# Regrouping the block-attention scores of layer 1: both chunks of a section in one group, later transposes

## The chip, the cores and the metric

The kernel runs on one core of a Trainium2 chip. The metric is the device time of one execution in microseconds, as the median over several runs. The engines are named as the profile names them: PE (TensorE matmul), PEld (its weight loads), DVE (VectorE), ACT (ScalarE), POOL (GpSimd), SP (SyncE, which issues the weight loads from memory).

## The reference

A decoder trunk of two layers on 256 positions of width 1024. Layer 0 mixes tokens by dilated sliding-window attention, layer 1 by MoBA block attention; each is followed by a gated feed-forward net with a causal convolution. The change is in layer 1's attention:

```python
SEQ = 256; N_HEADS = 16; HEAD_DIM = 64; MOBA_BLOCK = 256
def mixer_moba(h, w_qkv, q_gain, k_gain, w_o, cos, sin):
    qkv = (h @ w_qkv).reshape(B, S, 3, N_HEADS, HEAD_DIM)
    q = apply_partial_rope(rmsnorm(qkv[:, :, 0], q_gain), cos, sin)
    k = apply_partial_rope(rmsnorm(qkv[:, :, 1], k_gain), cos, sin)
    v = qkv[:, :, 2]
    ...
    s_own = jnp.einsum('hqd,hkd->hqk', qc, k_own) * ATTN_SCALE   # own block only: fully past blocks do not exist here
    s_own = jnp.where((kpos[None, :] <= qpos[:, None])[None], s_own, -jnp.inf)
    p = jax.nn.softmax(...)
    return o + jnp.einsum('hqk,hkd->hqd', p[..., n_sel:], v_own)
```

With 256 positions there is a single block of 256, so layer 1 is plain causal attention with 16 heads.

## The kernel before

**Tiling.** The positions form two chunks of 128 rows. The 16 heads are worked in four sections of four heads. Weights stream in as units; each unit is split by ACT into a rounded part `whi` (L109) and by DVE into the rest `wlo` (L117), and each product takes three matmuls of 128x512 (`mm3`, L456 to L458): x-high by `whi`, x-low by `whi`, x-high by `wlo`.

**Turns.** The program is an order written out by hand. `turn` runs one step `fn` of weight matmuls and, around it, what earlier steps have put into the tables `first`, `pre`, `mid` and `post` for this turn number. A turn issues, in this order: up to two `whi` splits, the entries of `first`, one `wlo`, the entries of `pre`, the other `wlo`, the matmuls of `fn`, the entries of `post`. `at(table, d, f)` puts `f` into the turn `d` later. Each engine executes its own instructions in the order in which they are issued. In the attention a turn has 12 weight matmuls, in the output projection of layer 1 (`out_proj`) 6.

**Buffers.** Tiles of one name share a fixed number of buffers: PSUM banks `S` 4, `acc` 3, `O` 1; in SBUF `sm` 2, `qk` 5, `pT` 4. A new tile takes the buffer that has been free longest, and its first writer waits for that buffer's last reader.

**One section of layer 1.** The product gives q and k of a chunk (`qk_block`); ACT squares and copies it (L539, L533), DVE sums and rotates (`head_sums`, `factors`), PE transposes it (`transpose`, L580), ACT copies it (L610) and DVE makes the low parts (`second_parts`, L616, L618). Then, for a group of heads of chunk `c`:

- `step_A`: score matmuls into two S banks (L676 for chunk 0, 128 keys; L682 for chunk 1, 256 keys)
- `step_E`: masked maxima (L708) and bias (L715) on DVE, exponentials on ACT (L717), into `sm`
- `step_R`: division by the sums on DVE (L722, L724)
- `step_T`: transposes on PE into S banks (L732); four for a group of 512 columns
- `step_V`: copies by ACT into `pT` (L739)
- `step_C`: matmuls with v into `O` for the whole section (L764); in the turn after, `split_T` brings `O` into `aT` as high part (ACT, L444) and low part (DVE, L445)

Chunk 0 is one group of four heads, chunk 1 two groups of two. Counted from layer 1's first turn, sections start in turns 0, 8, 12 and 16 and the output projection in turn 24. Scores of chunk 0 stand behind the matmuls of turns 6, 13, 18 and 23, those of chunk 1 in turns 8 and 10, 15 and 17, 20 and 22, 25 and 27. A group has its exponentials in the next turn, its transposes two turns after its scores (three in the last section), its `pT` copies in the turn after that. The values stand in turns 14, 21 and 26, and for the last section 28 (chunk 0) and 32 (chunk 1). The q/k transposes stand in turns 4, 7, 12, 14, 16, 18, 20 and 22. v of section 3 is copied by ACT (L646) at the end of turns 21 and 23. The `post` entries of one turn are sorted by kind only below turn 80 of the whole program, that is in layer 0.

Of the kernel before, what the change touches and what calls it, by code (L numbers as in the profile page):

```python
# [10 lines left out]
F32 = mybir.dt.float32  # L11
# [6 lines left out]
P = 128  # L18
# [9 lines left out]
HS = 4  # L28
SW = HS * HD
NSEC = NH // HS  # L30
# [8 lines left out]
PUMPS = (0, 0, 0, 1, 1, 1, 1, 1, 1, 1, 1, 1, 1, 0, 1, 1)  # L39

PART_TURNS = 80
PART = {"step_C": 0, "step_A": 1, "step_T": 2, "transpose": 3}

PLANS = (14, 24), (14, 20), (16, 24)

LATER = (0, 1), (2, 3)

C_TURN = (34, 30, 33)

V_TURN = {3: (0, 2), 1: (0, 3)}  # L50
OUT_UNITS = ((0, 0), (0, 1), (1, 0), (1, 1), (0, 2), (1, 2), (0, 3), (1, 3))
# [7 lines left out]
def r32(ap):  # L59
    return ap.bitcast(F32)  # L60
# [81 lines left out]
def trunk_kernel(ctx, tc, x, a_w_qkv, a_w_o, b_w_qkv, b_w_o, ffn_norm, ffn_w_up, ffn_w_down, pack, mask_a, mask_b,  # L142
# [4 lines left out]
    bp = ctx.enter_context(tc.tile_pool(name="bp", bufs=1))  # L147
# [64 lines left out]
    now = [0]  # L212
    first, pre, mid, post = {}, {}, {}, {}

    def at(table, dt, fn, *args):
        table.setdefault(now[0] + dt, []).append((fn, args))

    def turn(fn, pump=2, crowded=False):

        t = now[0]  # L220
        end = len(ws.parts) if t >= LATE else None
        n = min(pump, 1 if len(ws.parts) - ws.taken >= AHEAD else 2)
        if not crowded:
            ws.start(n)
        for f, a in first.pop(t, ()):
            f(*a)
        ws.finish(1, end)
        for f, a in pre.pop(t, ()):
            f(*a)
        if crowded:  # L230
            ws.start(n)
        ws.finish(end=end)
        if fn is not None:
            fn()

        late = post.pop(t, [])
        if t < PART_TURNS:
            late.sort(key=lambda fa: PART.get(fa[0].__name__, len(PART)))
        for f, a in late:
            f(*a)  # L240
        now[0] += 1
# [205 lines left out]
    def new_T():  # L447
        return cp.tile([P, 8, 2, S], F32R, name="xT", bufs=2)
# [12 lines left out]
    def attention(xT, norms, ng, g0, mask):  # L461


        dil = ng == 3
        moff = 3 * P if dil else P
        aT = new_T()

# [193 lines left out]
        O, weights, starts = {}, {}, []  # L661

        def step_A(sec, c, heads, qkT, v, rq):

            n = 3 * P if dil else (c + 1) * P
            cs = slice(c * P, (c + 1) * P)

            banks = [ps.tile([P, 512], F32, name="S", bufs=4) for _ in range(len(heads) if dil else 2)]
            place = [(banks[i], 0) if dil else (banks[i % 2], i // 2 * n) for i in range(len(heads))]
            todo = [(s2, o, slice(h % 2 * HD, h % 2 * HD + HD), h // 2) for (s2, o), h in zip(place, heads)]  # L670
            pairs = [todo[i:i + 2] for i in range(0, len(heads), 2)]
            for two in pairs:
                if not dil and c == 0:
                    t0 = qkT[0][0]
                    for s2, o, rows, pr in two:
                        nc.tensor.matmul(s2[:, o:o + n], r32(t0[rows, 0, pr]), r32(t0[rows, 1, pr]),  # L676
                                         start=True, stop=True)
                    continue
                q, kT = (qkT[0][0][:, :, :, cs], qkT[0][1]) if dil else qkT[0][1:]
                for a, b in ((0, 0), (1, 0), (0, 1)):  # L680
                    for s2, o, rows, pr in two:
                        nc.tensor.matmul(s2[:, o:o + S], q[rows, a, pr], kT[rows, pr, b],  # L682
                                         start=(a + b == 0), stop=(b == 1))
            for two in pairs if dil else ():
                for a in range(2):
                    r = slice(a * 64, (a + 1) * 64)
                    for j in range(2):
                        t = qkT[1 + (a + j) % 2][c]
                        for s2, o, rows, pr in two:
                            oj = o + S + j * 64  # L690
                            nc.tensor.matmul(s2[r, oj:oj + 64], r32(t[rows, 0, pr, r]), r32(t[rows, 1, pr, r]),
                                             start=True, stop=True)
            den, mx, nb_ = (sp.tile([P, 4], F32, name=t, bufs=2) for t in ("den", "mx", "nbias"))
            sm = []
            wide = dil and len(heads) > 2
            for i in (0, 2) if wide else (0,):
                at(pre if i and sec < NSEC - 1 else first, 1, step_E, c, heads, rq, place, n, slice(i, i + 2 if wide else len(heads)), sm, den, mx, nb_)
            at(first, 2, step_R, heads, sm, den, n)
            at(post, (2 if sec == NSEC - 1 else 4) if wide else 3 if not dil and sec == NSEC - 1 else 2, step_T, sec, c, heads, v, sm, n)

        def step_E(c, heads, rq, place, n, part, sm, den, mx, nb_):

            t = bp.tile([P, 768], F32, name="sm", bufs=2)
            these = range(len(heads))[part]
            sm.extend(t[:, i * n:(i + 1) * n] for i in range(len(these)))
            for i in these:
                s2, o = place[i]
                nc.vector.tensor_tensor_reduce(  # L708
                    out=sm[i], in0=s2[:, o:o + n], in1=mask[:, c * moff:c * moff + n],
                    op0=ALU.add, op1=ALU.max, scale=1.0, scalar=-3.0e38, accum_out=mx[:, i:i + 1])  # L710
            if dil:
                nc.vector.tensor_scalar_mul(nb_[:, part], mx[:, part], -1.0)
            else:
                f = rq[c][:, heads[these[0]]:heads[these[-1]] + 1]
                nc.vector.scalar_tensor_tensor(nb_[:, part], mx[:, part], -1.0, f, op0=ALU.mult, op1=ALU.mult)  # L715
            for i in these:
                nc.scalar.activation(sm[i], sm[i], AF.Exp, bias=nb_[:, i:i + 1],  # L717
                                     scale=1.0 if dil else rq[c][:, heads[i]:heads[i] + 1], accum_out=den[:, i:i + 1])
# [16 lines left out]
        def step_V(sec, c, heads, v, Tp, tot):  # L735
            pT = [bp.tile([P, 768], F32, name="pT", bufs=4) for _ in range((tot + 767) // 768)]
            cuts = sorted({*range(0, tot, 512), *range(0, tot, 768)}) + [tot]
            for o, e in zip(cuts, cuts[1:]):
                nc.scalar.activation(pT[o // 768][:, o % 768:o % 768 + e - o], Tp[o // 512][:, o % 512:o % 512 + e - o], AF.Copy)  # L739

            whole = sec < NSEC - 1
            key = sec if whole else (sec, c)
            held = weights.pop(key, []) + [(c, heads, pT, v)]
            if heads[-1] < HS - 1 and (whole or not dil) or whole and c == 0:
                weights[key] = held
            else:
                at(post, starts[sec] + C_TURN[sec] - now[0] if whole and dil else 1, step_C, sec, held)

        def step_C(sec, held):

# [19 lines left out]
        if dil:  # L770
            plan, odd, begin = ([(s, c, (0, 1, 2, 3)) for c, s in enumerate(p)] for p in PLANS)
            last = [(13, 0, (0, 1, 2, 3)), (16, 1, (0, 1, 2, 3))]
        else:
            plan, odd, last = ([(s, 0, (0, 1, 2, 3)), (s + 2, 1, (0, 1)), (s + 4, 1, (2, 3))] for s in (6, 5, 7))
        pumps = PUMPS if dil else (2, 0, 0, 2, 1, 2)
        vs = [[None, None] for _ in range(NSEC)]
        for sec in range(NSEC):
            qk, v, rq = [], vs[sec], {}
            starts.append(now[0])
            for s, c, heads in last if sec == NSEC - 1 else begin if dil and sec == 0 else odd if sec % 2 else plan:  # L780
                at(post, s, step_A, sec, c, heads, qk, v, rq)
            dones = [qk_block(sec, g, qk, rq) for g in range(ng)]
            if dil and sec == 0:
                gens = [opening(dones), product(dones[2], "S")]
            else:
                gens = [product(d) for d in dones]
            gens += [v_first(v)] if dil else []
            gens += [v_last(vs[sec // 2 * 2:sec // 2 * 2 + 2])] if sec in V_TURN[ng] else []
            fns = [fn for gen in gens for fn in gen]
            if sec == 0:  # L790
                fns[0:5] = [fns[i] for i in (range(5) if dil else (0, 1, 4, 2, 3))]
            for i, fn in enumerate(fns):
                turn(fn, pumps[i] if sec == 0 and i < len(pumps) else 2, dil and sec == NSEC - 1 and i > 12)
# [228 lines left out]
    at(post, 12, nc.sync.dma_start, pk[:, 264:PK], pack[:, 264:PK])  # L1022
    at(post, 20, nc.sync.dma_start, mB, mask_b)
    aT = attention(xT, norms, NG, 0, mA)
    for c in range(2):
        nc.gpsimd.dma_start(xr[:, c, :], x[0, c * P:(c + 1) * P, :])
# [109 lines left out]
```

## Time and profile before

| | |
|---|---|
| median of 3 runs | 763.05 us (762.54 to 763.41) |
| span of the profiled execution, first to last instruction | 760.9 us |
| the profiled execution's own time | not on record beside its span; the span is 2.15 us under the median |
| TensorE clock granted | 1.000 |
| PE busy | 756.4 us, 99% |
| DVE busy | 582.3 us, 77% |
| ACT busy | 506.0 us, 67% |
| moved from and to memory | 133.83 MB, 176 GB/s on average |

Busy times are sums over an engine's instructions. Matmuls are pipelined and their lengths overlap (a 128x512 matmul is shown as 390 ns long), so distances between starts are what tells PE's pace. An idle time stands in brackets behind an instruction, with what ended it.

### The profile page before, as it was taken

What the parts mean: (1) busy time and instruction counts of PE and PEld (TensorE: products, weight loads), DVE (VectorE), ACT (ScalarE), POOL (GpSimd) and SP (SyncE); (2) the same over time, 40 slices, a digit from 0 to 9 for tenths busy, and PEclk for the clock granted to TensorE, in tenths of its full rate; (3) what the DMA queues carried; (4) which work ended last, traced back from release to release, by engine and by line L of the source; (5) the groups of instructions that cost most, each with busy time, mean ns of one, the idle gap of its engine ahead of it and who ended that gap; (6) DMA issues with size and microseconds to landing.
All of it is one profiled execution on the core that took longest, in us unless ns stands there. A gap on an engine that the chain in (4) does not pass through costs nothing.

```text
span 760.9 us, 12046 instructions
## 1 busy us (share of the span) xinstructions
PE 756.4 (99%) x4394; PEld 635.4 (84%) x4394; DVE 582.3 (77%) x1123; ACT 506.0 (67%) x887; POOL 69.8 (9%) x77
## 2 busy tenths in 40 slices
PE   9999999999999999999999999999999999999998
PEld 8888888888888888888888888787778888888886
DVE  6887875975786566997887787978866798877874
ACT  7778666757776457676666656777765677566660
POOL 0330120320131000000000001112000000000000
PEclk9999999999999999999999999999999999999999
DMA  9947462562746436487666553743646368666621
GB/s 293 332 141 251 132 186 80 181 217 65 231 158 223 132 90 194 146 251 215 192 193 183 195 190 116 231 139 112 190 116 185 119 186 247 200 178 200 191 100 56
DMA packets 149452, 133.83 MB, mean 176 GB/s; under 512 B 5904, under 2 KB 134544, under 8 KB 149392
## 3 DMA queue, kind: packets, MB, share of 16 engines
q1 hardware_dynamic: 148816, 130.96, 56.0%
q0 software_dynamic: 576, 2.10, 0.7%
q8 instruction: 34, 0.56, 0.3%
q14 instruction: 26, 0.21, 0.1%
HBM read 131.99 MB, written 1.05 MB: 175 GB/s over the span
## 4 chain that ended last, share of the span: by engine, by line
PE 99%; DVE 0%; issue 0%
PE acc L887 14%; PE acc L456 13%; PE acc L458 13%; PE acc L457 13%; PE acc L890 8%; PE S L940 5%; PE S L941 5%; PE S L942 5%; PE O L887 5%; PE O L890 3%; PE O L764 2%; PE acc L513 2%; PE S L732 2%; PE acc L580 2%; PE S L682 2%; PE O L513 1%
## 5 line engine op out<-in xcount | busy, mean ns | idle before, releaser
L117 DVE TENSOR_TENSOR wlo<-raw,whi 128x1024 fp32r<-128x1024 f32 x236 | 283.5, 1217 | 7.0 <-ACT whi L109 6.6
L109 ACT ACTIVATE whi<-raw 128x1024 fp32r<-128x1024 f32 x236 | 244.3, 1054 | 5.7 <-DMA raw<-in_a_w_qkv_dram 2.3
L456 PE MATMUL acc<-whi,xT 128*128 128x512 f32 x424 | 171.8, 405 | 0.0
L458 PE MATMUL acc<-wlo,xT 128*128 128x512 f32 x424 | 165.8, 391 | 0.0
L457 PE MATMUL acc<-whi,xT 128*128 128x512 f32 x424 | 165.4, 390 | 0.0
L887 PE MATMUL acc<-xT,whi 128*128 128x512 f32 x480 | 119.3, 390 | 0.0
L887 PEld LDWEIGHTS acc<-xT,whi 128*128 128x128 f32 x480 | 88.3, 188 | 17.2
L458 PEld LDWEIGHTS acc<-wlo,xT 128*128 128x128 f32 x424 | 79.6, 188 | 17.5
L456 PEld LDWEIGHTS acc<-whi,xT 128*128 128x128 f32 x424 | 79.7, 188 | 16.8 <-issue 1.2
L457 PEld LDWEIGHTS acc<-whi,xT 128*128 128x128 f32 x424 | 79.9, 188 | 14.7
L318 POOL TENSOR_TENSOR rs_y<-rs_v,mhalf 128x8 f32<-128x8 f32 x32 | 53.7, 1681 | 210.9 <-DVE rs_v L316 208.0
L890 PEld LDWEIGHTS acc<-xT,wlo 128*128 128x128 f32 x480 | 65.5, 190 | 4.7
L940 PE MATMUL S<-whi,kT 128*128 128x512 f32 x174 | 68.2, 392 | 0.0
L941 PE MATMUL S<-whi,kT 128*128 128x512 f32 x174 | 68.1, 391 | 0.0
L942 PE MATMUL S<-wlo,kT 128*128 128x512 f32 x174 | 67.7, 389 | 0.0
L890 PE MATMUL acc<-xT,wlo 128*128 128x256 f32 x480 | 66.9, 282 | 0.0
L911 DVE SCALAR_TENSOR_TENSOR qk<-sm,pk,qk 128x255 f32<-128x255 f32 (+1 forms) x160 | 66.6, 476 | 0.4 <-ACT qk L908 0.3
L900 DVE TENSOR_TENSOR sm<-acc,pT 128x256 f32<-128x256 f32 x60 | 25.4, 423 | 46.9 <-ACT pT L899 46.9
L908 ACT ACTIVATE qk<-sm,pk 128x256 f32<-128x256 f32 x80 | 47.8, 598 | 4.0 <-DVE sm L900 3.7
L924 ACT ACTIVATE kT<-qk 128x512 fp32r<-128x512 f32 x22 | 13.9, 633 | 41.2 <-DVE qk L919 41.2
L887 PE MATMUL O<-xT,whi 128*128 128x512 f32 x160 | 40.2, 393 | 0.0
L942 PEld LDWEIGHTS S<-wlo,kT 128*128 128x128 f32 x174 | 32.7, 188 | 7.0
(167 smaller groups left out, 927.5 us busy)
## 6 DMA issues: line engine op xcount, KB each, us to landing
raw<-in_ffn_w_up_dram SPq DMA_DIRECT2D x80, 512.0 KB, 4.2
raw<-in_a_w_qkv_dram SPq DMA_DIRECT2D x144, 256.0 KB, 4.3
raw<-in_ffn_w_down_dram SPq DMA_DIRECT2D x44, 512.0 KB, 3.8
raw<-in_b_w_qkv_dram SPq DMA_DIRECT2D x48, 256.0 KB, 3.5
raw<-in_a_w_o_dram SPq DMA_DIRECT2D x8, 512.0 KB, 3.8
raw<-in_ffn_w_up_dram SPq DMA_DIRECT2D x16, 256.0 KB, 3.6
raw<-in_b_w_o_dram SPq DMA_DIRECT2D x8, 512.0 KB, 3.8
xr<-in_x_dram POOLq DMA_DIRECT2D x2, 512.0 KB, 5.9
```

Of the source, the lines that this page charges most:

```text
L109: self.nc.scalar.activation(hi, raw, AF.Copy)
L117: self.nc.vector.tensor_sub(lo, self.raw[self.done], r32(hi))
L318: nc.gpsimd.tensor_tensor(y, v, mhalf[:, 0:n], op=ALU.pow)
L456: nc.tensor.matmul(acc, T[:, k, 0, cs], hi, start=first, stop=False)
L457: nc.tensor.matmul(acc, T[:, k, 1, cs], hi, start=False, stop=False)
L458: nc.tensor.matmul(acc, T[:, k, 0, cs], lo, start=False, stop=last)
L887: nc.tensor.matmul(acc, hi[:, k], xT[:, k].rearrange("p j t -> p (j t)"), start=(k == 0), stop=False)
L890: nc.tensor.matmul(acc[:, S:2 * S], lo[:, k], xT[:, k, 0], start=False, stop=(k == 7))
L911: nc.vector.scalar_tensor_tensor(o[:, d:S], u[:, 0:S - d], cw[:, first_tap + b:first_tap + b + 1], o[:, d:S], op0=ALU.mult, op1=ALU.add)
L940: nc.tensor.matmul(o, acts[f][:, 0, cs], hi[:, sl], start=start, stop=False)
L941: nc.tensor.matmul(o, acts[f][:, 1, cs], hi[:, sl], start=False, stop=False)
L942: nc.tensor.matmul(o, acts[f][:, 0, cs], lo[:, sl], start=False, stop=stop)
```

## The change

In layer 1 the scores of both chunks of a section are issued together (`step_AB`) in turn 8, 15 and 20, for sections 0 to 2; chunk 1's four heads are one group; the values of a section follow at fixed turns (15, 20 and 25), in two cases right behind the next section's scores, and the entries of `post` are now sorted in all turns from 80 on by a second table: scores, values, transposes, q/k transposes. Section 3 keeps its chunks apart (turns 23 and 25), with chunk 1 as one group of four heads; its values stand in turns 28 and 30. The exponentials of chunk 0 come in the next turn; those of chunk 1 in two halves, in sections 0 to 2 the first in `pre` of the next turn and the second in `first` of the turn after it. The transposes of sections 0 to 2 come three turns (chunk 0) and four turns (chunk 1) after the scores: turns 11 and 12, 18 and 19, 23 and 24; those of section 3 in turns 26 and 28. Chunk 0's softmax tile in sections 0 to 2 is now a `qk` buffer. Chunk 1's eight transposes take two S banks, and its `pT` data two `pT` buffers.

```diff
-PART = {"step_C": 0, "step_A": 1, "step_T": 2, "transpose": 3}
+PART = {"step_C": 0, "step_A": 1, "step_T": 2, "transpose": 3}, {"step_AB": 0, "step_A": 0, "step_C": 1, "step_T": 2, "transpose": 3}
-C_TURN = (34, 30, 33)
+C_TURN = (34, 30, 33), (15, 12, 13)
+
+BOTH = 8, 7, 8
...
         late = post.pop(t, [])
-        if t < PART_TURNS:
-            late.sort(key=lambda fa: PART.get(fa[0].__name__, len(PART)))
+        order = PART[t >= PART_TURNS]
+        late.sort(key=lambda fa: order.get(fa[0].__name__, len(order)))
...
-            for i in (0, 2) if wide else (0,):
-                at(pre if i and sec < NSEC - 1 else first, 1, step_E, c, heads, rq, place, n, slice(i, i + 2 if wide else len(heads)), sm, den, mx, nb_)
-            at(first, 2, step_R, heads, sm, den, n)
-            at(post, (2 if sec == NSEC - 1 else 4) if wide else 3 if not dil and sec == NSEC - 1 else 2, step_T, sec, c, heads, v, sm, n)
-
-        def step_E(c, heads, rq, place, n, part, sm, den, mx, nb_):
-
-            t = bp.tile([P, 768], F32, name="sm", bufs=2)
+            if dil:
+                when = [(pre if i and sec < NSEC - 1 else first, 1) for i in ((0, 2) if wide else (0,))]
+                dr, dt = 2, (2 if sec == NSEC - 1 else 4) if wide else 2
+            elif sec == NSEC - 1:
+                when, dr, dt = ([(first, 1), (pre, 1)], 2, 3) if c else ([(first, 1)], 2, 3)
+            else:
+                when, dr, dt = ([(pre, 1), (first, 2)], 3, 4) if c else ([(first, 1)], 2, 3)
+            step = len(heads) // len(when)
+            for i, (table, d) in enumerate(when):
+                at(table, d, step_E, sec, c, heads, rq, place, n, slice(i * step, (i + 1) * step), sm, den, mx, nb_)
+            at(first, dr, step_R, heads, sm, den, n)
+            at(post, dt, step_T, sec, c, heads, v, sm, n)
+
+        def step_AB(sec, qkT, v, rq):
+
+            for c in range(2):
+                step_A(sec, c, (0, 1, 2, 3), qkT, v, rq)
+
+        def step_E(sec, c, heads, rq, place, n, part, sm, den, mx, nb_):
+
+            t = bp.tile([P, 768], F32, name="sm", bufs=2) if dil or c or sec == NSEC - 1 else bp.tile([P, 512], F32, name="qk", bufs=5)
...
-            if heads[-1] < HS - 1 and (whole or not dil) or whole and c == 0:
+            if whole and c == 0:
                 weights[key] = held
             else:
-                at(post, starts[sec] + C_TURN[sec] - now[0] if whole and dil else 1, step_C, sec, held)
+                at(post, starts[sec] + C_TURN[l][sec] - now[0] if whole else 1, step_C, sec, held)
...
-            plan, odd, last = ([(s, 0, (0, 1, 2, 3)), (s + 2, 1, (0, 1)), (s + 4, 1, (2, 3))] for s in (6, 5, 7))
+            last = [(7, 0, (0, 1, 2, 3)), (9, 1, (0, 1, 2, 3))]
...
-            for s, c, heads in last if sec == NSEC - 1 else begin if dil and sec == 0 else odd if sec % 2 else plan:
-                at(post, s, step_A, sec, c, heads, qk, v, rq)
+            if not dil and sec < NSEC - 1:
+                at(post, BOTH[sec], step_AB, sec, qk, v, rq)
+            else:
+                for s, c, heads in last if sec == NSEC - 1 else begin if sec == 0 else odd if sec % 2 else plan:
+                    at(post, s, step_A, sec, c, heads, qk, v, rq)
```

More of the change, by code (lines that the diff above doesn't have):

```diff
@@ L464, in attention @@
         dil = ng == 3
+        l = 0 if dil else 1
         moff = 3 * P if dil else P
```

## Prediction, made before the change was run

> **What bounds the kernel now.** I read the page first, then layer 1's attention (from 468 us on) engine by engine in the timeline.
>
> ```profile
> span 760.9 us, 12046 instructions
> ...
> PE 756.4 (99%) x4394; PEld 635.4 (84%) x4394; DVE 582.3 (77%) x1123; ACT 506.0 (67%) x887; POOL 69.8 (9%) x77
> ```
>
> PE is busy over practically the whole span, so time can be won only by giving PE less to do and is lost wherever PE is made to wait. The span lies 2.15 us under the median of the runs, 763.05 us; the profiled execution has no other time on record, so I form the sum as a difference in PE's time and add it to the median.
>
> The PE timeline, one stretch of layer 0 and two of layer 1 (start, length, instruction; lengths overlap, so I use start to start):
>
> ```profile
> 115.61 0.98 PE L682 MATMUL S<-kT 64*128 64x256 f32 x12
> 116.51 0.74 PE L691 MATMUL S<-t 64*64 64x64 f32 x32
> ...
> 502.04 0.39 PE L457 MATMUL acc<-whi,xT 128*128 128x512 f32 x1
> 502.26 0.39 PE L458 MATMUL acc<-wlo,xT 128*128 128x512 f32 x1
> 502.58 0.71 PE L676 MATMUL S<-t 64*128 64x128 f32 x8
> 503.23 0.50 PE L456 MATMUL acc<-whi,xT 128*128 128x512 f32 x1
> 503.56 0.39 PE L457 MATMUL acc<-whi,xT 128*128 128x512 f32 x1
> ...
> 510.71 0.39 PE L458 MATMUL acc<-wlo,xT 128*128 128x512 f32 x1
> 511.03 0.62 PE L682 MATMUL S<-kT,t 64*128 64x256 f32 x6
> 511.58 0.65 PE L732 MATMUL S<-ident,sm 128*128 128x128 f32 x4
> 511.99 0.47 PE L456 MATMUL acc<-whi,xT 128*128 128x512 f32 x1
> 512.30 0.39 PE L457 MATMUL acc<-whi,xT 128*128 128x512 f32 x1
> ```
>
> A weight matmul follows its predecessor after 0.22 to 0.23 us. Each interruption costs more than its own matmuls: 0.32 instead of 0.23 ahead of the first score matmul (502.26 to 502.58), 0.33 instead of 0.23 behind it (503.23 to 503.56); about 0.18 together. The pieces themselves: chunk 0's scores 0.65, half of chunk 1's scores 0.55, four transposes 0.41.
>
> ACT and DVE, which set when PE may go on:
>
> ```profile
> 530.85 0.47 ACT L610 ACTIVATE kT<-acc,gqk 128x256 fp32r<-128x256 f32 x1
> ...
> 531.85 1.07 ACT L109 ACTIVATE whi<-raw 128x1024 fp32r<-128x1024 f32 x1
> ...
> 536.88 0.37 ACT L444 ACTIVATE xT<-O 128x256 fp32r<-128x256 f32 x1
> 537.74 0.38 ACT L444 ACTIVATE xT<-O 128x256 fp32r<-128x256 f32 x1 [0.49 <-DVE xT L445]
> ...
> 540.26 2.00 ACT L109 ACTIVATE whi<-raw 128x1024 fp32r<-128x1024 f32 x2
> 542.15 0.59 ACT L717 ACTIVATE sm<-sm,nbias,rs_y 128x256 f32<-128x256 f32 x1
> ...
> 543.32 0.59 ACT L739 ACTIVATE pT<-S 128x512 f32<-128x512 f32 x1
> 543.80 0.69 ACT L646 ACTIVATE v<-acc,rn_r 128x512 f32<-128x512 f32 x1
> 544.37 1.06 ACT L109 ACTIVATE whi<-raw 128x1024 fp32r<-128x1024 f32 x1
> 545.43 0.49 ACT L717 ACTIVATE sm<-sm,nbias,rs_y 128x128 f32<-128x128 f32 x1
> ...
> 547.36 1.05 ACT L109 ACTIVATE whi<-raw 128x1024 fp32r<-128x1024 f32 x1
> 548.31 0.57 ACT L739 ACTIVATE pT<-S 128x512 f32<-128x512 f32 x1
> ```
>
> ```profile
> 538.16 0.42 DVE L445 TENSOR_TENSOR xT<-O,xT 128x256 fp32r<-128x256 f32 x1 [0.45 <-ACT xT L444]
> 538.50 1.22 DVE L117 TENSOR_TENSOR wlo<-raw,whi 128x1024 fp32r<-128x1024 f32 x1
> 539.63 0.42 DVE L708 CUSTOM_DVE_ANT_0 sm<-S,mB 128x256 f32<-128x256 f32 x1
> ...
> 540.43 0.16 DVE L715 SCALAR_TENSOR_TENSOR nbias<-mx,rs_y 128x2 f32<-128x2 f32 x1
> ```
>
> Prices from these, start to next start: three copies behind a q/k transpose 1.00 (530.85 to 531.85); one `whi` 0.95 (half of 540.26 to 542.15); two exponentials of chunk 1 1.17 (542.15 to 543.32); a `pT` copy 0.48; a `v` copy 0.57; four exponentials of chunk 0 1.93 (545.43 to 547.36); `split_T` of both chunks 1.70 (536.88 to 538.16 + 0.42), because ACT's second half waits for DVE's first and DVE's for ACT's; one `wlo` 1.13; the maxima and bias of two heads 0.96 (539.63 to 540.43 + 0.16).
>
> **The change part by part.** Turns are counted from layer 1's first turn, as above.
>
> *Fewer interruptions (gain).* No matmul is removed. Turns with anything behind the weight matmuls go from 24 (4, 6, 7, 8, 10, all of 12 to 28, 30 and 32, by the turns of the scores, transposes, q/k transposes and values) to 18 (4, 7, 8, 11, 12, 14, 15, 16, 18, 19, 20, 22 to 26, 28, 30). Six edges at 0.18 are 1.1 us; the few slower starts that follow an edge (0.23 to 0.24 instead of 0.227) add some 0.2. Chunk 1's scores stand together four times: twelve matmuls of this shape took 0.90 in layer 0 (115.61 to 116.51), two halves 2 x 0.55, so 0.2 at best and nothing at worst each time: I take 0.15, 0.6 in all. Gain 1.9 us, between 1.1 and 2.1.
>
> *The moved vector work (loss).* Nothing is added on ACT and DVE either, but it arrives in lumps. Both are read in program order, so what counts is the queue. The place where it bites is from turn 20 to the end of section 2. There turn 20 now issues both chunks' scores of section 2, then section 1's values, then the q/k transpose of section 3's chunk 0. ACT's copies of that transpose are issued in the same turn, ahead of turn 21's work; so ACT stands idle until PE has done the whole group, and then has everything of section 2 still before it. Before, section 2's chunk 0 had its exponentials in turn 19.
>
> I set zero at the start of that transpose. PE from there to section 3's chunk-1 scores (turn 25): transpose 0.4, turn 21's twelve weight matmuls 2.8 (12 x 0.227 and an edge), turn 22's 2.8, transpose 0.4, turn 23's 2.8, scores 0.65, transposes of section 2 chunk 0 0.4, turn 24's six 1.45 (out_proj's turns hold half as many), eight transposes 0.8, turn 25's six 1.45: **13.95 us**.
>
> ACT from there, in program order, with DVE where ACT waits for it: transpose done 0.6; three copies 1.00 (1.6); turn 21's `whi` 0.95 (2.55); four exponentials 1.93 (4.5); `split_T` of section 1 1.70 (6.2); on DVE the second part of kT, priced as the 0.42 of the equal-sized `lo` (6.6), `wlo` 1.13 (7.75), maxima and bias of chunk 1's first pair 0.96 (8.7); exponentials 1.17 (9.9); `v` 0.57 (10.45); turn 22's second pair 1.17 (11.6) and two copies 0.65 (12.3); turn 23's two `whi` 1.9 (14.2) and `v` 0.57 (14.75); turn 24's `whi` 0.95 (15.7), section 3 chunk 0's exponentials 1.93 (17.6), the `pT` copy of section 2 chunk 0 0.57 (**18.2**).
>
> That last copy frees the S bank that section 3's chunk-1 scores take: the ring of four is full because the merged group and the eight transposes hold it. PE is short of it by 18.2 - 13.95 = 4.3 us. Part of this will be paid earlier, at turn 24's eight transposes (one of their two banks is section 3 chunk 0's, and that chunk's `sm` buffer is itself freed only by the first half of those transposes); the sum stays. Even with a free bank the values of section 2 in turn 25 need the `pT` copies behind the same queue, so the 4.3 does not hang on the bank.
>
> Then section 2's chunk-1 `pT` copies: `whi` 0.95 and three copies 1.1 (512 columns 0.48, two of half the size an estimated 0.3 each) after 18.2 give 20.3; PE with scores 0.95 and chunk 0's values 0.5 is there at 19.65: 0.6 more. Then section 3's values in turn 28: behind section 2's values come `split_T` 1.70, `wlo` 1.13, maxima 0.96, exponentials 1.17, `pT` 0.57 = 5.5, against PE's 1.45 + 0.4 + 1.4 + 1.45 = 4.7: 0.8 more. Waits 5.7 us; I take 6.0, since semaphore steps between engines are not in it (some ten crossings).
>
> *The bound of the waits.* From below: if each crossing and each queue ran 5% faster than the rows, 18.2 shrinks by 0.9 and the two later ones vanish: 3.4. From above: 5% slower plus 0.1 per crossing, and a wait for an `acc` bank at turn 22's q/k transpose: 9. Turns 8 to 19 I cost at nothing: there PE has twelve weight matmuls in each turn and the transposes stand three and four turns behind their scores instead of two.
>
> [...] In the rows PE goes from one S bank's work to the next without a wait, each score piece holding two of four banks. [...]
>
> *Costed at nothing:* chunk 0's tile from the qk pool instead of sm (five buffers, none late); the sort in turns 80 and up outside the attention (no two such pieces share a turn); SP's and POOL's queues (weight loads and normalisation are issued where they were). The diff puts the second chunk's last two heads' exponentials two turns on, not one, in sections 0 to 2.
>
> **Sum:** -1.9 + 6.0 = +4.1; median 763.05 + 4.1 = **767.2 us**.
>
> **Rivals.**
> *The queues keep up (faster).* If ACT reached the `pT` copy of section 2 chunk 0 by 13.95 instead of 18.2, only the gain would be left: 763.05 - 1.9 = 761.2. For it: ACT is busy 67% over the span. Against it: the total of queued ACT and DVE work in that stretch is longer than PE's path, whatever the mean. It decides when more than 4 of the 18.2 us lie elsewhere. [...] Chance 0.08.
> *Waits and gain cancel.* Should the split's ping-pong (1.70) and the turn-23 `whi` lie earlier than I order them, waits of some 2 us are left: 763.0, within 0.2%. Chance 0.10.
> *A longer wait at turn 22.* Its q/k transpose needs an `acc` bank. I read it as the one of the transpose of turn 20, free at 6.6 when PE comes at 6.0. If it is turn 21's `v` bank, free only at 10.45, PE stands 4.4 us there, some 2 of which it saves later: 767.2 + 2.4 = 769.6. Chance 0.12.
> *My forecast.* Chance 0.70.
>
> **How the numbers follow.** 0.2% of this time is 1.5 us, about what can be told from no change. Slower: 0.70 + 0.12 = 0.82; same 0.10; faster 0.08. The range reaches from the cancelling case, 763.4, to the bound from above, 771.0 (waits 9, gain 1.1); the forecast's own is 764.4 (waits 3.4, gain 2.1) to 769.6.
>
> **What would show it.** Right: PE has idle time in front of the L682, L732 or L764 pieces between turns 22 and 28, released by ACT's `pT` copies (L739) or DVE, 4 us or more in all; layer 1's q/k transposes and merged scores show no new idle before turn 20; ACT sits idle some 3 us ahead of the L610 copies of turn 20. Wrong: PE stays at 99% with no idle above 0.5 us there, and the span drops. The gain is right if the attention of layer 1 without those waits is 1.1 to 2.1 us shorter.

## The result, and the profile after

The kernel with the change takes **768.57 us** (median of 4 runs, 766.90 to 768.78), the kernel before beside it 762.79 us (762.42 to 763.41): ratio **1.0069, 95% interval 1.0055 to 1.0084**, so 5.8 us slower. The forecast was 767.2 us, slower.

Lines of the page of the changed kernel that answer to those of before: the span is 6.1 us longer (767.0 against 760.9), while the busy time of PE, DVE and ACT has hardly moved. The work is the same; the order in which it stands costs time.

```profile
span 767.0 us, 12051 instructions
...
PE 756.1 (99%) x4394; PEld 637.1 (83%) x4394; DVE 581.4 (76%) x1119; ACT 506.5 (66%) x891; POOL 69.8 (9%) x77
```

The PE timeline of the changed kernel in layer 1's attention: every instruction that has idle time ahead of it (in brackets, with what ended it), two merged pieces without a wait, and rows behind the last wait. The diff has moved the line numbers: L583 are the q/k transposes, L685 chunk 1's scores, L748 the softmax transposes, L780 the values, L458 to L460 the weight matmuls.

```profile
520.68 0.66 PE L583 MATMUL acc<-ident,qk 128*128 128x128 f32 x4 [0.76 <-DVE kT L621]
...
528.11 1.21 PE L685 MATMUL S<-kT,t 64*128 64x256 f32 x12
529.24 1.53 PE L780 MATMUL O<-pT,v 128*64 128x128 f32 x24
...
537.50 0.63 PE L583 MATMUL acc<-ident,qk 128*128 128x128 f32 x4 [0.65 <-DVE kT L621]
...
545.36 0.66 PE L748 MATMUL S<-ident,sm 128*128 128x128 f32 x4 [1.42 <-DVE mx L724]
...
549.05 0.97 PE L685 MATMUL S<-kT,t 64*128 64x256 f32 x11 [1.34 <-ACT pT L755]
549.95 1.72 PE L780 MATMUL O<-pT,v 128*64 128x128 f32 x24
...
551.60 0.50 PE L458 MATMUL acc<-whi,xT 128*128 128x512 f32 x1
...
558.57 0.66 PE L780 MATMUL O<-pT,v 128*64 128x128 f32 x8 [2.11 <-ACT pT L755]
...
561.28 0.63 PE L459 MATMUL acc<-whi,xT 128*128 128x512 f32 x1
561.71 0.63 PE L460 MATMUL acc<-wlo,xT 128*128 128x512 f32 x1
...
563.10 0.40 PE L458 MATMUL acc<-whi,xT 128*128 128x512 f32 x1
563.34 0.39 PE L459 MATMUL acc<-whi,xT 128*128 128x512 f32 x1
```

Five waits, in turns 18, 22, 24, 25 and 28, together 6.28 us (0.76 + 0.65 + 1.42 + 1.34 + 2.11). The kernel before has none from 515 to 570 us. Behind the last wait the weight matmuls follow each other at 0.43 us (561.28 to 561.71), some rows later again at 0.24 (563.10 to 563.34): for a while PE ran at half its pace. The stretches of the changed kernel show the same in the granted clock (the last three columns are clock, DMA share, GB/s):

```profile
core 0: us, PE busy (x) PEld busy (x) DVE busy (x) ACT busy (x) POOL busy (x), PEclk, DMA share, GB/s
550.00:555.00 5.00, 5.00 (x42) 4.14 (x42) 2.82 (x9) 2.90 (x9) 0.00 (x0) 1.00 0.77 217
555.00:560.00 5.00, 2.89 (x19) 2.12 (x18) 3.19 (x12) 2.97 (x7) 0.00 (x0) 0.93 0.39 110
560.00:565.00 5.00, 5.00 (x25) 3.97 (x26) 1.32 (x2) 1.25 (x3) 0.00 (x0) 0.73 0.36 105
565.00:570.00 5.00, 5.00 (x33) 4.10 (x28) 1.81 (x3) 1.72 (x5) 0.00 (x0) 1.00 0.01 3
```

The clock was 0.07 short over 5 us and 0.27 short over the next 5: 5 x 0.07 + 5 x 0.27 = 1.7 us lost. Of the four runs three have a granted clock of 0.998 (768.49 to 768.78 us), one 1.000: 766.90 us. So the balance of the spans is 6.28 (waits) + 1.7 (clock) - gain = 6.1, which leaves a gain of 1.9 us.

Why PE waits is in the ACT timeline and, below it, the DVE timeline of the changed kernel:

```profile
531.40 0.47 ACT L613 ACTIVATE kT<-acc,gqk 128x256 fp32r<-128x256 f32 x1 [3.11 <-PE acc L583]
...
539.48 0.60 ACT L733 ACTIVATE sm<-sm,nbias,rs_y 128x256 f32<-128x256 f32 x1 [2.98 <-DVE rd L738]
...
548.41 0.59 ACT L755 ACTIVATE pT<-S 128x512 f32<-128x512 f32 x1
...
551.77 0.60 ACT L733 ACTIVATE sm<-sm,nbias,rs_y 128x256 f32<-128x256 f32 x1 [0.81 <-DVE nbias L731]
...
552.96 0.36 ACT L446 ACTIVATE xT<-O 128x256 fp32r<-128x256 f32 x1
```

```profile
518.93 0.41 DVE L724 CUSTOM_DVE_ANT_0 sm<-S,mB 128x256 f32<-128x256 f32 x1
...
520.14 0.48 DVE L621 SCALAR_TENSOR_TENSOR kT<-acc,gqk,kT 128x256 fp32r<-128x256 f32 x1
...
535.66 0.42 DVE L447 TENSOR_TENSOR xT<-O,xT 128x256 fp32r<-128x256 f32 x1 [3.55 <-ACT xT L446]
536.53 0.42 DVE L447 TENSOR_TENSOR xT<-O,xT 128x256 fp32r<-128x256 f32 x1 [0.45 <-ACT xT L446]
536.88 0.47 DVE L621 SCALAR_TENSOR_TENSOR kT<-acc,gqk,kT 128x256 fp32r<-128x256 f32 x1
537.27 1.22 DVE L119 TENSOR_TENSOR wlo<-raw,whi 128x1024 fp32r<-128x1024 f32 x1
```

From turn 20 to 22: ACT idles 3.11 us until PE has gone through the merged group; then DVE idles 3.55 us for ACT's first half of section 1's `split_T`, which stands behind four exponentials; then ACT idles 2.98 us for DVE. The second part of kT (L621), which frees the bank of PE's next q/k transpose, stands behind the split. Two engines busy 66% and 76% of the span take turns in waiting for each other, and PE pays.

### The profile page after: what moved, and what is told of

It reads as the page before. It is cut to its first block, busy times and chain, and to the rows that moved or that the text cites. A ratio compares the mean times of both kernels' runs of the same rounds, so it can differ in the third digit from the quotient of the medians.

```text
span 767.0 us, 12051 instructions
## 1 busy us (share of the span) xinstructions
PE 756.1 (99%) x4394; PEld 637.1 (83%) x4394; DVE 581.4 (76%) x1119; ACT 506.5 (66%) x891; POOL 69.8 (9%) x77
## 4 chain that ended last, share of the span: by engine, by line
PE 96%; ACT 2%; DVE 1%; issue 0%; ACTq 0%
PE acc L906 14%; PE acc L458 12%; PE acc L460 12%; PE acc L459 12%; PE acc L909 7%; PE S L959 5%; PE S L960 5%; PE S L961 5%; PE O L906 5%; PE O L909 2%; PE acc L516 2%; PE O L780 2%; PE S L748 2%; PE acc L583 2%; PE S L685 1%; ACT sm L733 1%
## 5 line engine op out<-in xcount | busy, mean ns | idle before, releaser
L458 PE MATMUL acc<-whi,xT 128*128 128x512 f32 x424 | 171.6, 405 | 0.0
L460 PE MATMUL acc<-wlo,xT 128*128 128x512 f32 x424 | 166.0, 392 | 0.0
L460 PEld LDWEIGHTS acc<-wlo,xT 128*128 128x128 f32 x424 | 79.8, 188 | 17.6
L458 PEld LDWEIGHTS acc<-whi,xT 128*128 128x128 f32 x424 | 79.9, 189 | 16.2 <-issue 0.9
L459 PEld LDWEIGHTS acc<-whi,xT 128*128 128x128 f32 x424 | 80.1, 189 | 14.9
L447 DVE TENSOR_TENSOR xT<-O,xT 128x256 fp32r<-128x256 f32 x16 | 8.4, 522 | 44.1 <-ACT xT L446 44.1
```

The source lines that it names most:

```text
L458: nc.tensor.matmul(acc, T[:, k, 0, cs], hi, start=first, stop=False)
L459: nc.tensor.matmul(acc, T[:, k, 1, cs], hi, start=False, stop=False)
L460: nc.tensor.matmul(acc, T[:, k, 0, cs], lo, start=False, stop=last)
```

## The experiments

Clock values are those granted over a whole run. The kernel before stood at 762.50 us (9 runs) beside the first four kernels, 762.79 (18 runs) beside the next four, 762.65 (17 runs) beside the last three.

**Section 1's values one turn later** (turn 21 instead of 20, so no longer in the merged group of turn 20):

```diff
-C_TURN = (34, 30, 33), (15, 12, 13)
+C_TURN = (34, 30, 33), (15, 13, 13)
```

> The changed kernel with section 1's values in turn 21 instead of turn 20 (and their split_T a turn later with them); nothing else moves, no buffer is added. Queue theory (ACT and DVE run their work in issue order; the lump behind turn 20's long group makes them late, and DVE waits in front of split_T while wlo and the maxima stand behind it): PE's waits between turns 18 and 28 fall from 6.3 us to about 4.3 us, the ones ahead of the q/k transpose of turn 22 and part of the later ones go; 766 to 767 us. Bank theory (PE waits because the merged group and the eight transposes hold all four S banks, in the same order as before): the same banks are asked for in the same order, so the waits at turns 24 and 25 stay at 1.4 and 1.3 us and at most the one of turn 22 goes: 768 us.

Measured 765.53 us (765.35 to 766.89), ratio 1.0043 (1.003 to 1.0057). At clock 1.000 it is 1.4 us under the changed kernel (765.47 against 766.90). Its waits in the PE timeline:

```profile
520.73 0.66 PE L583 MATMUL acc<-ident,qk 128*128 128x128 f32 x4 [0.76 <-DVE kT L621]
...
544.23 0.66 PE L748 MATMUL S<-ident,sm 128*128 128x128 f32 x4 [0.81 <-DVE mx L724]
...
547.25 0.97 PE L685 MATMUL S<-kT,t 64*128 64x256 f32 x11 [0.67 <-ACT pT L755]
...
556.78 0.66 PE L780 MATMUL O<-pT,v 128*64 128x128 f32 x8 [2.13 <-ACT pT L755]
```

The wait of turn 22 is gone, those of turns 24 and 25 have halved (1.42 and 1.34 to 0.81 and 0.67): 4.37 us in all instead of 6.28. The waits of turns 22 to 25 are in good part one debt, made in turns 20 to 22.

**Values left in turn 20, only section 1's split a turn later:**

```diff
-                    at(first, 1, split_T, aT, sec * 2, 2, c, O[sec, c][:, c], dil)
+                    at(first, 2 if not dil and sec == 1 else 1, split_T, aT, sec * 2, 2, c, O[sec, c][:, c], dil)
```

> The changed kernel with only section 1's split_T a turn later (turn 22 instead of 21); all PE work stays where it is. Queue theory: DVE's idle time of 3.6 us in front of the first low part goes, the maxima of section 2's second chunk come some 3 us earlier, the waits fall by about 2 us: 766 to 767 us, as with the values moved. If PE's order in turn 20 (scores, then values, then the q/k transpose) were the cause, nothing would change: 768.5 us.

Measured 766.53 us (765.58 to 767.05), ratio 1.0052 (1.0039 to 1.0064); 765.58 in the one run at clock 1.000. Waits 0.76, none in turn 22, 0.97, 0.67, 2.14: 4.54 us. PE's program is that of the changed kernel here, and the wait of turn 22 is gone all the same. So what PE waited for there was the split in the queues of ACT and DVE, not the length of its own group.

**A bank borrowed from `acc`:** section 3's chunk-1 scores get their second bank from `acc` and need not wait for the `pT` copy that frees an S bank.

```diff
-            banks = [ps.tile([P, 512], F32, name="S", bufs=4) for _ in range(len(heads) if dil else 2)]
+            banks = [ps.tile([P, 512], F32, name="S", bufs=4) for _ in range(len(heads) if dil else 2 if (sec, c) != (3, 1) else 1)]
+            if not dil and (sec, c) == (3, 1):
+                banks.append(new_acc())
```

> The changed kernel with one of the two banks for section 3's chunk-1 scores (turn 25) taken from acc, which has a free one there, instead of S. Bank theory: the 1.3 us ahead of those scores go and the time falls by as much, to about 767.2 us. Queue theory: the scores start at once, but the values right behind them wait for the pT copies that stand in the same ACT queue; the wait moves to L780 and the time stays at 768.2 to 768.6 us.

Measured 767.21 us (766.87 to 767.31), ratio 1.006 (1.0048 to 1.0073). Its PE timeline from turn 25 on:

```profile
549.28 0.66 PE L782 MATMUL O<-pT,v 128*64 128x128 f32 x8 [0.74 <-ACT pT L757]
550.71 1.19 PE L782 MATMUL O<-pT,v 128*64 128x128 f32 x16 [0.77 <-ACT pT L757]
...
556.76 0.50 PE L458 MATMUL acc<-whi,xT 128*128 128x512 f32 x1 [1.45 <-DVE mx L726]
...
558.81 0.66 PE L782 MATMUL O<-pT,v 128*64 128x128 f32 x8 [0.40 <-ACT pT L757]
```

The scores no longer wait, the values behind them do (0.74 + 0.77), and in turn 28 the output projection waits for the borrowed bank (1.45) and the values for 0.40. All waits together are 6.19 us against 6.28: the free bank moved them and took nothing away. At clock 1.000 the time is that of the changed kernel (four runs, 766.87 to 767.31, against 766.90); the lower median goes with the clock, which stayed at 1.000 in four runs of five; the fifth has 0.998 and, at 766.92 us, was no slower. The longest wait is 1.45 us instead of 2.11.

**The queue loaded further:** two ACT copies of 128x512, whose results nothing uses, at the start of turn 21, in the changed kernel and in the kernel before.

```diff
+        def extra():
+            for _ in range(2):
+                nc.scalar.activation(sp.tile([P, 512], F32, name="sq", bufs=2), xr[:, 0, 0:512], AF.Copy)
...
+            if not dil and sec == 3:
+                at(first, 5, extra)
```

> The changed kernel with two more ACT copies of 128x512 (about 1.0 us together, into a scratch tile nobody reads) at the start of turn 21. Queue theory: ACT is on the path there, so the time grows by 0.7 to 1.0 us, to about 769.4 us, with the waits ahead of turns 22 to 25 longer. If ACT had slack there: no change.

> The kernel before with the same two ACT copies of 128x512 (about 1.0 us) at the start of turn 21. Queue theory: before the change ACT idles 1.7 us in that turn waiting for DVE, so nothing reaches PE: 762.5 us, within 0.3 us. If ACT's total work were what bounds this stretch in both kernels: 763.5 us.

In the changed kernel: 769.57 us (768.17 to 769.89), ratio 1.0089 (1.0075 to 1.0103); at clock 1.000 it is 768.17 against 766.90, so 1.27 us for 1.15 us of ACT work. In the kernel before: 762.88 us (11 runs), ratio 1.0001 (0.9992 to 1.001), nothing. PE of the changed kernel with the copies, turn 22:

```profile
538.19 0.63 PE L583 MATMUL acc<-ident,qk 128*128 128x128 f32 x4 [1.68 <-DVE kT L621]
```

The wait of 0.65 became 1.68. ACT of the kernel before in the same turn, without the copies, then with them:

```profile
534.65 0.60 ACT L717 ACTIVATE sm<-sm,nbias,rs_y 128x256 f32<-128x256 f32 x1 [1.73 <-DVE nbias L715]
```

```profile
533.18 1.15 ACT L663 ACTIVATE sq<-xr 128x512 f32<-128x512 f32 x2
535.01 0.60 ACT L721 ACTIVATE sm<-sm,nbias,rs_y 128x256 f32<-128x256 f32 x1 [0.68 <-DVE nbias L719]
```

There the copies fit into ACT's idle time (1.73 to 0.68). In the changed kernel ACT's queue in turns 20 to 22 is PE's critical path; in the kernel before it is not.

**Section 3's chunk-0 tile from the `qk` pool,** alone and together with the later values:

```diff
-            t = bp.tile([P, 768], F32, name="sm", bufs=2) if dil or c or sec == NSEC - 1 else bp.tile([P, 512], F32, name="qk", bufs=5)
+            t = bp.tile([P, 768], F32, name="sm", bufs=2) if dil or c else bp.tile([P, 512], F32, name="qk", bufs=5)
```

> The changed kernel with section 3 chunk 0's softmax tile from the qk buffers instead of sm, so that its maxima no longer wait for section 2's transposes to free an sm buffer. Queue theory: DVE is not free for these maxima any earlier, so no change: 766.9 us at full clock, 768.5 us where the clock drops. If the two sm buffers were the cause of the 1.4 us inside the eight transposes of turn 24: about 1.2 us less.

> The changed kernel with both: section 1's values in turn 21, and section 3 chunk 0's softmax tile from qk. Queue theory: with the queue 2 us less late, the sm buffer becomes what section 3's maxima wait for, so the two together take away more than the sum, the waits at turns 24 and 25 go from 0.8 and 0.7 us to about 0.4 us in all, the one at turn 28 stays: 764.5 us at full clock. If the tile is irrelevant here too: 765.4 us as with the values alone.

Alone: 768.88 us (767.13 to 769.80), ratio 1.0074 (1.0062 to 1.0087), and the waits of the changed kernel to 0.03 us. So the `sm` buffer did not hold turn 24's transposes at that point. Together with the later values: 765.87 us (765.67 to 766.11), ratio 1.004 (1.0028 to 1.0053); the wait of turn 24, 0.81 with the later values alone, is gone, and 0.76, 0.66 and 2.08 are left. The buffer was the next limit behind the queue. It lies 1.4 us over the expected time, which had no loss of clock in it; the clock was 0.998 in all five runs.

**The groups kept, the moved work spread:** values of section 0 in turn 16 and of section 1 in 21; splits of sections 0 and 2 a turn later; in sections 0 and 2 both halves of chunk 1's exponentials in the next turn, as section 3 has them; transposes of section 1's chunk 1 and section 2's chunk 1 a turn earlier, those of section 3 in turns 25 and 29, its values in 29 and 31; the `qk` tile.

```diff
-C_TURN = (34, 30, 33), (15, 12, 13)
+C_TURN = (34, 30, 33), (16, 13, 13)
...
-                when, dr, dt = ([(first, 1), (pre, 1)], 2, 3) if c else ([(first, 1)], 2, 3)
+                when, dr, dt = ([(first, 1), (pre, 1)], 2, 4) if c else ([(first, 1)], 2, 2)
...
-                when, dr, dt = ([(pre, 1), (first, 2)], 3, 4) if c else ([(first, 1)], 2, 3)
+                when, dr, dt = (([(first, 1), (pre, 1)], 2, 4), ([(pre, 1), (first, 2)], 3, 3), ([(first, 1), (pre, 1)], 2, 3))[sec] if c else ([(first, 1)], 2, 3)
...
-                at(post, starts[sec] + C_TURN[l][sec] - now[0] if whole else 1, step_C, sec, held)
+                at(post, starts[sec] + C_TURN[l][sec] - now[0] if whole else 1 if dil else (3, 1)[c], step_C, sec, held)
...
-                    at(first, 1, split_T, aT, sec * 2, 2, c, O[sec, c][:, c], dil)
+                    at(first, 2 if not dil and sec in (0, 2) else 1, split_T, aT, sec * 2, 2, c, O[sec, c][:, c], dil)
```

> A version meant to keep the groups and lose the waits: section 0's values in turn 16 and section 1's in 21, split_T of sections 0 and 2 a turn later, chunk 1's exponentials in the next turn in all sections, section 3 chunk 0 in a qk tile and its transposes in turn 25, its values in 29, section 3 chunk 1's transposes in 29 and values in 31. Queue theory: waits of PE in the attention fall below 0.5 us and the gain from fewer interruptions is left: 762.5 - 1.6 = 760.9 us, full clock. If grouping itself does not save PE time: 762.5 us or more.

Measured **760.74 us** (8 runs, 760.44 to 761.64), ratio **0.9974 (0.9964 to 0.9985)**: faster than both kernels, clock 1.000 in all runs. PE waits left in its attention:

```profile
541.35 0.66 PE L748 MATMUL S<-ident,sm 128*128 128x128 f32 x4 [0.27 <-DVE mx L724]
...
552.56 0.50 PE L459 MATMUL acc<-whi,xT 128*128 128x512 f32 x1 [0.36 <-DVE xT L447]
```

The merged groups were not what cost time; where their followers stood was. Since all these moves were made at once, the share of each is not shown.

**The clock by itself:** the kernel before, not regrouped, with 3, 5 and 8 unused ACT copies ahead of the split and the `pT` copy that section 3's first values wait for. Each makes one PE wait in the attention and no other. The edit with three copies; the others have 5 and 8 in its place:

```diff
+        def extra():
+            for _ in range(3):
+                nc.scalar.activation(sp.tile([P, 512], F32, name="sq", bufs=2), xr[:, 0, 0:512], AF.Copy)
...
+            if not dil and sec == 3:
+                at(first, 11, extra)
```

> The kernel before, its order unchanged, with three added ACT copies of 128x512 at the start of turn 27, ahead of the split of section 2's second chunk and of the pT copy that section 3's first values wait for. The copies' results are used by nothing. Three copies at the 0.48 us of a pT copy are 1.45 us; in the kernel before that pT copy ends some 0.5 us ahead of PE, so one PE wait of about 0.9 us ahead of the values. Theory (the granted clock falls for a fixed dose of 1.7 us only after a PE wait of about 2 us, whatever made it): granted clock 1.000, 762.8 + 0.9 = 763.7 us. Rival (the loss of clock belongs to the grouped order, or to several waits in a row): the same here, and it parts from the theory at the five and eight copies. Second rival (the loss grows with the wait, some 0.8 us per us waited): 764.4 us with a granted clock under 1.000.

> As with three copies, but five: 2.4 us on ACT, one PE wait of about 1.9 us. Theory: the wait is about at the length at which the clock fell in the changed kernel (2.1 us), so in some or all executions the granted clock is 0.998: 764.7 us without and 766.4 us with the dose of 1.7 us. Rival (it belongs to the grouped order or to four earlier waits): clock 1.000 always, 764.7 us. Second rival (it grows with the wait): 766.2 us always.

> As with three copies, but eight: 3.85 us on ACT, one PE wait of about 3.4 us. Theory: the dose is fixed, 1.7 us, and is paid in every execution: 762.8 + 3.4 + 1.7 = 767.9 us, granted clock 0.998. Rival (it belongs to the grouped order or to four earlier waits): 766.2 us at clock 1.000. Second rival (it grows with the wait): 762.8 + 3.4 + 2.7 = 768.9 us, granted clock about 0.996.

Measured, against 762.65 us: 763.36 us with three copies (10 runs; 1.001, 1.0001 to 1.002), 764.56 with five (8 runs; 1.0025, 1.0015 to 1.0036), 767.67 with eight (4 runs; 1.0067, 1.0052 to 1.0082). The one PE wait of each, and its stretch of 10 us:

```profile
555.27 0.66 PE L768 MATMUL O<-pT,v 128*64 128x128 f32 x8 [0.70 <-ACT pT L743]
```

```profile
556.33 0.66 PE L768 MATMUL O<-pT,v 128*64 128x128 f32 x8 [1.74 <-ACT pT L743]
```

```profile
554.00:564.00 10.00, 8.26 (x57) 6.47 (x55) 5.42 (x14) 6.05 (x16) 0.00 (x0) 1.00 0.31 85
```

```profile
558.10 1.12 PE L768 MATMUL O<-pT,v 128*64 128x128 f32 x8 [3.30 <-ACT pT L743]
```

```profile
554.00:564.00 10.00, 6.70 (x33) 5.22 (x32) 4.03 (x12) 6.85 (x16) 0.00 (x0) 0.83 0.18 48
```

Waits of 0.70 and 1.74 us cost 0.71 and 1.91 us, themselves and hardly more. The wait of 3.30 us cost 5.02: itself and 1.7, which is the clock of 0.83 over 10 us. Four runs of four paid it (clock 0.997 to 0.998). The rival by which the loss belongs to the grouped order (766.2 us) falls; that it grows with the wait falls too, since 1.74 us cost no clock, and 3.30 us the same 1.7 as 2.11 us did. With five copies the theory left open whether the clock would fall; it did not.

## Why the prediction was right, and where it was off

*The bound, and the mechanism.* Right. PE stayed at 99% and lost its time by waiting, in the places named but for turn 18, released by `pT` copies or DVE; a loss of clock, not foreseen, came on top. ACT sat idle 3.11 us ahead of turn 20's copies (some 3 were forecast). Loading ACT's queue, shifting the split and shifting the values each moved the waits as the queue argument says.

*The queue to turn 25.* ACT's chain was right almost to the tenth: from turn 20's transpose to the end of section 2's first `pT` copy 18.2 us were forecast; the transpose starts at 530.77 (row of the chain of waits below) and the copy ends at 549.00. PE's own way was not: 549.05 - 530.77 less the waits of 3.4 is 14.9 us, against 13.95. So the waits of turns 22, 24 and 25 are 3.4 us where 4.3 were put. Of the extra some 0.4 us is one score matmul that ran ahead of the wait (the row behind it counts 11 of 12) and 0.2 the eight transposes, which their wait cuts in two; the rest is about 0.1 in each of three stretches of weight matmuls. Turn 22's part, read as 6.6 against 6.0, came out at 0.65: the bank was the one of turn 20's transpose, and the rival with the `v` bank falls.

```profile
530.77 0.60 PE acc L583 x4
531.40 0.47 ACT kT L613
```

*Section 2's values,* 0.6: not seen as a wait. Their 24 matmuls take 1.72 us where section 1's took 1.53, and none shows idle time ahead of it: 0.2 at most.

*Turn 28,* 0.8: **mis-sized**, it measured 2.11. The steps from split to `pT` copy were summed as 5.5 and took 5.6 (split from 552.96, copy released PE at 558.57). But the split did not start behind the values, which PE had done at 551.6: ahead of it ACT's queue held the first pair of section 3's chunk-1 exponentials, which the sum had left out (the ACT rows at 551.77 and 552.96). This is read from the rows; no run moves that pair alone.

*Turns 8 to 19 at nothing:* wrong by 0.76. In turn 18 the q/k transpose waits for the second part of kT, which on DVE stands behind maxima of the merged group (the DVE rows at 518.93 and 520.14); the wait is there in every regrouped kernel that keeps section 0's plan and gone in the one that spreads it. Which of the moves in section 0 removes it was not tried alone.

*The gain,* 1.9: by subtraction 1.9. The same balance (span, less waits, less 1.7 us where the clock fell, against 760.9) gives 1.7 to 2.4 us in the seven other regrouped kernels. The scores give more of it than the 0.6 put there, as the merged group of turn 8 shows:

```profile
484.81 0.71 PE L679 MATMUL S<-t 64*128 64x128 f32 x8
485.27 0.96 PE L685 MATMUL S<-kT,t 64*128 64x256 f32 x12
486.16 0.50 PE L458 MATMUL acc<-whi,xT 128*128 128x512 f32 x1
```

The twelve chunk-1 matmuls take 0.89 us where two halves took 1.10, and the eight of chunk 0, with chunk 1's right behind them, 0.46 instead of 0.65. The group of turn 15 is alike (1.36 in all); that of turn 20 takes 1.60, since its twelve need 1.13 (the PE rows at 528.11 and 529.24). Against 1.75 for the pieces of the kernel before, the three groups save 0.9 us. What the removed edges give was not measured by itself. The 0.18 us of an edge holds for scores (64*128 in the rows); around transposes, whose rows have 128*128 like those of the weight matmuls, the second start is nearly as dear (0.31 in the kernel before, 526.23 to 526.54), the first is not (0.24, 525.64 to 525.88). What makes these starts dearer is not shown.

*Left out:* the clock. No step of the prediction had the 1.7 us that most runs pay behind the wait of turn 28. That the waits came to 6.28 us for 6.0 is in part luck, since their errors were of both signs: turns 22 to 25 priced 1.5 us too high with section 2's values, turns 18 and 28 some 2.1 too low. Two smaller numbers of the prediction do not hold either. No run shows the 0.1 us per crossing in its upper bound: in the changed kernel's chain of waits it is 0.01 to 0.05 us from the end on one engine to the start on the next (530.77 + 0.60 to 531.40 above: 0.03). And the cancelling case stands once at 763.0 and once at 763.4, where -1.9 + 2 gives 763.15. Without the clock the forecast would have been 0.3 us high, with it 1.4 us low.

*The borrowed bank.* A bank borrowed from `acc` was worth nothing (767.21 us, and 766.87 to 767.31 at clock 1.000 against 766.90): the `pT` copies that the values need stood behind the same queue, and the output projection then waited 1.45 us for the bank lent. A bank more in all was not tried.

## What to carry to other kernels

Where one engine is busy nearly all the time and two others serve it from in-order queues, sum the queue of each helper in program order from the last point at which it idled, count every instruction that stands ahead (the pair left out in turn 28 cost more than the whole term had been priced at), and set it against the bound engine's way to the same point. When a regrouping makes such waits, move the followers (values, splits, halves of exponentials) before giving up the groups: the same groups gave +5.8 us in one order and -2.0 us in another. Cut the longest wait first: here a TensorE wait of 1.74 us cost 1.91 us, itself and hardly more; longest waits of some 2.1 us cost 1.7 us extra in 21 of 28 runs, one of 3.30 us in 4 of 4.

## What the runs showed of the hardware that was not expected

The loss of clock came in one size. A longest PE wait of 1.74 us: none in 8 runs. About 2.1 us (the changed kernel and the five experiments that keep turn 28's wait): a clock of 0.998 in 21 of 28 runs. 3.30 us: 0.997 to 0.998 in 4 of 4. The dose is 1.7 us in each of the six traces that have one: their windows give 5 x 0.07 + 5 x 0.27 (changed kernel), 5 x 0.24 + 5 x 0.10 (later values), 5 x 0.21 + 5 x 0.13 (later split), 5 x 0.34 (two copies in the changed kernel, and later values with the `qk` tile), and 10 x 0.17 (eight copies). With weight matmuls at 0.43 instead of 0.23 us, that is some 3.4 us at half pace. The kernel with the borrowed bank has 6.19 us of waits, none over 1.45; one of its five runs shows a clock of 0.998 all the same, without a longer time and without a trace, and stays open.

In the traces it is not the length of the wait alone that goes with a drop, but how much of it falls into one stretch of 3.413 us. The clock record of the changed kernel's trace is 1.000 for 552.96 us, 0.500 for 3.413 us and 1.000 for the next 204.80 us: 162, 1 and 60 such stretches. The next rows cut three traces along this grid, from the start of each trace's first clock record: first the changed kernel, then the later values with the `qk` tile, then the `qk` tile alone. Ahead of the same values the kernels have a wait of 2.11, 2.08 and 2.08 us (columns as above; PE's busy time comes first, the clock third from the end).

```profile
555.86:559.27 3.41, 1.30 (x12) 0.71 (x11) 1.94 (x10) 2.51 (x6) 0.00 (x0) 1.00 0.54 154
559.27:562.69 3.42, 3.42 (x13) 3.03 (x14) 1.71 (x3) 1.72 (x5) 0.00 (x0) 0.50 0.02 6
562.69:566.10 3.41, 3.41 (x27) 2.55 (x26) 0.00 (x0) 0.37 (x1) 0.00 (x0) 1.00 0.50 148
```

```profile
552.29:555.70 3.41, 1.33 (x8) 0.79 (x6) 2.00 (x9) 1.85 (x6) 0.00 (x0) 1.00 0.43 127
555.70:559.11 3.41, 3.41 (x18) 2.98 (x19) 2.38 (x6) 2.23 (x5) 0.00 (x0) 0.50 0.11 32
```

```profile
553.45:556.86 3.41, 3.08 (x16) 2.24 (x13) 2.83 (x8) 0.44 (x2) 0.00 (x0) 1.00 0.33 97
556.86:560.28 3.42, 1.67 (x17) 1.50 (x18) 1.79 (x7) 3.24 (x8) 0.00 (x0) 1.00 0.51 153
560.28:563.69 3.41, 3.41 (x26) 2.64 (x26) 1.08 (x1) 0.82 (x3) 0.00 (x0) 1.00 0.29 80
```

In the first two, all 2.11 and 2.08 us of waiting lie in one stretch, and the next stretch runs at half clock. In the third, the wait is split into 0.33 and 1.75 us, and the clock stays. Nor did it fall with five copies, whose whole wait is 1.74 us. Only one run of each kernel has a trace; that the place of the grid also parts the other runs into those with a dose and those without would fit, but is not shown.
